# The order of two block products in the feed-forward input units of a two-layer attention and mLSTM kernel

## The chip, the cores and the metric

The kernel runs on one core of a Trainium2 chip. The metric is the device time of one execution in microseconds; less is better. The engines are named as the profile names them: PE is the matrix engine (PEld its weight load), DVE the vector engine, ACT the scalar engine, POOL GpSimd, and SP the engine that issues most DMAs. Matmuls read SBUF and accumulate into PSUM banks; ACT and DVE read the banks.

## The reference

The model has a dilated attention layer and an mLSTM layer over 512 tokens of width 1024, each followed by a gated feed-forward block. The block is what the change touches:

```python
D_FF = -(-8 * D_MODEL // (3 * 256)) * 256        # 2816

def swiglu(xn, w_in, w_out):
    gu = xn @ w_in
    return (jax.nn.silu(gu[..., :D_FF]) * gu[..., D_FF:]) @ w_out

def reference(x, positions, ...):
    h = x
    for i in range(DEPTH):                       # 2
        ...                                      # attention, then mLSTM
        h = h + swiglu(rms_norm(h, ffn_norm[i]), ffn_w_in[i], ffn_w_out[i])
    return rms_norm(h, final_norm)
```

All is in float32, and nothing of the change alters what is computed; the sums of one unit are only formed in another order.

## The kernel before, in words

One program runs the layers one after the other. Names beginning with `f0` and `f1` are the feed-forward input of layer 0 and 1, `o0` and `o1` the out-projections behind them. A float32 product is made of three matmuls of shorter numbers: every operand is split into a high part (`_h`, ACT, L207) and a low part (`_l`, DVE, L208), and high by high, low by high and high by low are added up in the bank.

`ffn_in` computes silu(x w_gate) * (x w_up). After a rest of 256 columns (`f0rest`) come five units, u = 0 to 4, of 512 gate and 512 up columns. The tokens are cut into two halves, and the weights of a unit into four blocks: a11 and a12 make the gate columns, a21 and a22 the up columns, each from one half of the input width. Instead of eight block products a unit has seven, after the manner of Strassen: `PRODUCTS` lists them in the order of their issue. Four of them use sums of weight blocks (s1 to s4, their splits are named `f00s`, the first digit after f being the layer and the next the unit), and T1 to T4 are sums of token blocks that are made once in each layer.

A product is two chunks c of 256 input rows, and in each the two 128-token tiles t, with 6 matmuls for each t: 24 matmuls of 128x512 outputs. Three pairs of PSUM banks, one bank for each t, collect them:

- "c": a11, then a12.
- "p": s1, then s4.
- "u": begun with a copy of a11's sum by ACT (L1222), then s2, s3 and a22.

Only a11 and s1 start their banks anew. Each later product adds on top of what stands there, and each partial sum is wanted by itself. So the sum must be read off a bank before the next product on the same bank may write. `after` does this when a product's last chunk is done: s1 leaves `up` (copy by ACT, L1214), s2 leaves `g2` (copy by ACT, L1214, named `g` in the trace), s4 is folded onto `g2` (DVE, L1217) which then goes through silu (ACT, L1235), s3 is folded onto `up` (DVE, L1217) which is multiplied by `g2` (DVE, L1239) and, in units 0 to 3, transposed in 32x32 blocks by DVE into a tile named `turn` (L1183). The sum after a22 goes with the gate of a12 the same way (L1243). `turn` is then spread into the hidden tile (`hid`): twelve small DMAs by SP (L1194) and four copies by POOL (L1199), which POOL makes after the second L1130 DMA of the next unit.

Weights come in raw tiles two chunks ahead of their products (`AHEAD`, `prepare`). Two tiles per chunk, `first` (block a11) and `own` (a21, onto which POOL's DMA adds a22, L1103), carry all four sums: DVE adds `first` to `own` after the split for s1 (L1129), POOL's accumulating DMA adds a21 to `first` (L1130), which is then s3's operand, and DVE adds a12 to `own` (L1134), which is then s4's. Each tag has two buffers, so the loads of the next unit wait for the last reader of the tiles.

Unit 4 has no `turn`: its rows are turned by PE in the out-projection. `early` does the out-projection's first steps during unit 4, after the products s2, the next two, and a22: B11 forms of the hidden tiles, split by ACT (L1371, `o0B`) and DVE (L1373). Further steps (DVE L1427, ACT L1408) are also put among unit 4's.

Within each engine the order of instructions is fixed when the program is built, by a scheduler that follows the order of the code and its own estimates. So moving a product moves the instructions around it as well.

Of the kernel before, what the change touches and what calls it, by code (L numbers as in the profile page):

```python
# [15 lines left out]
ALU = mybir.AluOpType  # L16
# [54 lines left out]
def tile_hybrid_dilated_attn_mlstm(  # L71
# [4 lines left out]
    nc = tc.nc  # L76
# [64 lines left out]
    def advance():  # L141
        tick[0] += 1
        run_deferred(lambda t: t <= tick[0])
# [200 lines left out]
    with ExitStack() as actx:  # L344
# [62 lines left out]
        banks = [("s", 2), ("s", 2), ("acc", 3), ("acc", 3), ("acc", 3), ("t", 1), ("s", 2), ("s", 2)]  # L407
# [321 lines left out]
        kept = dp.tile([KC, P, SEQ], F32, name="x_kept")  # L729
# [338 lines left out]
        return pair, rbc, r, hook  # L1068


    PRODUCTS = (("a11", "B11"), ("a12", "B21"), ("s1", "T1"), ("s2", "T2"), ("s4", "B22"), ("s3", "T3"), ("a22", "T4"))
    UNITS = D_FF // 512
    AHEAD = 2

# [4 lines left out]
    def ffn_in(layer, fp, x1, x2, pair, r, nr, unit):  # L1079
# [6 lines left out]
        todo = [("rest", None, c) for c in range(KC // 2)] + [  # L1086
            (u, key, c) for u in range(UNITS) for key, _ in PRODUCTS for c in range(2)]
        made, raw, toks = {}, {}, {}
# [78 lines left out]
        def tokens(okey, part, k, t):  # L1167
            if okey[0] == "T":
                return toks[okey][part][:, k, t * P:(t + 1) * P]
            c0 = HALF * (int(okey[2]) - 1) + t * P  # L1170
            return pair[part][4 * (int(okey[1]) - 1) + k][:, c0:c0 + P]

        def bank(tag, bufs, name):
            return ps.tile([P, 512], F32, tag=tag, name=nm + name, bufs=bufs)

        def wide(tag, name, n=512, p=fp):
            return p.tile([P, 512], F32, tag=tag, name=nm + name, bufs=2)[:, :n]
# [9 lines left out]
        def spread(dest, src):  # L1187
            for a, g in itertools.product(range(TB), repeat=2):
                to = dest[32 * g:32 * g + 32, :, a * P:(a + 1) * P]
                of = src[32 * a:32 * a + 32, g].rearrange("p n o j -> p n (o j)")  # L1190
                if a == g:
                    waiting.append((to, of))
                else:
                    nc.sync.dma_start(to, of)  # L1194
# [18 lines left out]
        def after(u, key, banks, t, kept):  # L1213
            copy = lambda to, src, scale: nc.scalar.activation(to, src, AF.Copy, scale=scale)  # L1214

            def fold(to, src, scale):
                nc.vector.scalar_tensor_tensor(to, src, scale, to, op0=ALU.mult, op1=ALU.add)  # L1217
            o = 2 + t
            if key == "a11":
                if t == 0:  # L1220
                    banks["u"] = [bank("o", 2, "u%d_u" % u) for _ in range(2)]
                nc.scalar.activation(banks["u"][t], banks["c"][t], AF.Copy)  # L1222
            elif key == "a12":
                g = kept["g", t] = wide("sq", "u%dg%d" % (u, t), p=npl)
                nc.scalar.activation(g, banks["c"][t], AF.Silu, scale=r[:, t:t + 1])
            elif key == "s1":
                kept["up", t] = wide("up", "u%dup%d" % (u, o))
                copy(kept["up", t], banks["p"][t], nr[:, o:o + 1])
            elif key == "s2":
                kept["g2", t] = wide("g2", "u%dg%d" % (u, o))  # L1230
                copy(kept["g2", t], banks["u"][t], r[:, o:o + 1])
            elif key == "s4":
                g = kept["g2", t]
                fold(g, banks["p"][t], r[:, o:o + 1])
                nc.scalar.activation(g, g, AF.Silu)  # L1235
            elif key == "s3":
                up = kept["up", t]
                fold(up, banks["u"][t], nr[:, o:o + 1])
                nc.vector.tensor_tensor(up, up, kept["g2", t], op=ALU.mult)  # L1239
                store(u, o, up, kept)  # L1240
            else:
                g = kept["g", t]
                nc.vector.scalar_tensor_tensor(g, banks["u"][t], nr[:, t:t + 1], g, op0=ALU.mult, op1=ALU.mult)  # L1243
                store(u, t, g, kept)
                if t == 1 and u < UNITS - 1:
                    dest = fp.tile([P, 4, SEQ], F32, tag="hid%d" % u, name="%shid%d" % (nm, u))
                    hid[2 * u:2 * u + 2] = dest[:, 0:2], dest[:, 2:4]
                    spread(dest, kept["to"])

        def store(u, o, src, kept):  # L1250
            if u == UNITS - 1:
                unit.rows[o] = src
            else:
                if "to" not in kept:
                    kept["to"] = turned(4, "u%dturn" % u)
                turn(kept["to"], o, src, 4)
# [4 lines left out]
        for n, (u, key, c) in enumerate(todo):  # L1261
            prepare(n + AHEAD)
            whl = made.pop(n)
            if u == "rest":
                for o in range(TB):
                    for k in range(2):
                        for a, b in SPLITS:
                            nc.tensor.matmul(accs[o], pair[a][2 * c + k][:, o * P:(o + 1) * P], whl[b][:, k],  # L1268
                                             start=((c, k) == (0, 0) and (a, b) == SPLITS[0]),
                                             stop=((c, k) == (KC // 2 - 1, 1) and (a, b) == SPLITS[-1]))  # L1270
                if c == KC // 2 - 1:
                    rest_out(accs)
            else:
                if (key, c) == ("a11", 0):
                    banks, kept = {}, {}
                name = {"a11": "c", "a12": "c", "s1": "p", "s4": "p"}.get(key, "u")
                fresh = name not in banks
                if fresh:
                    banks[name] = [bank(*{"c": ("acc", 3), "p": ("s", 2)}[name], "u%d_%s" % (u, name)) for _ in range(2)]
                new = key in ("a11", "s1")  # L1280
                for t in range(2):
                    for k in range(2):
                        for a, b in SPLITS:
                            nc.tensor.matmul(banks[name][t], tokens(dict(PRODUCTS)[key], a, 2 * c + k, t), whl[b][:, k],  # L1284
                                             start=(new and (c, k) == (0, 0) and (a, b) == SPLITS[0]),
                                             stop=((c, k) == (1, 1) and (a, b) == SPLITS[-1]), skip_group_check=True)
                if c == 1:
                    for t in range(2):
                        after(u, key, banks, t, kept)
                    if u == UNITS - 1:  # L1290
                        unit.early([k for k, _ in PRODUCTS].index(key))
            advance()
# [684 lines left out]
```

## Time and profile before

| | |
|---|---|
| time, median of 3 runs | 1393.19 us (1391.07 to 1393.89) |
| time of the profiled execution | 1393.05 us |
| its span | 1391.3 us |
| mean granted PE clock | 0.996 |
| PE busy | 1368.8 us (98%) |
| DVE, ACT, POOL busy | 1070.5, 712.4, 221.7 us |
| units of layer 0, of layer 1 | about 500 to 711 us, 1048 to 1269 us |

The span is what the profile shows of the execution; the time includes what lies around it. A row of a timeline reads: start, duration, engine, line, operation, output <- inputs, with the idle time before it and what ended that in brackets. A row of the wait view reads: who waited for whom, us in total, times, longest. A row of the window view reads: stretch, its length, busy time (and instructions) by engine, the granted PE clock (1.00 is full), the busy share of the DMA engines, GB/s.

### The profile page before, as it was taken

The page shows a single profiled execution, that of the slowest core. Times are in us where ns is not written, and L with a number is a line of the kernel's source. Part 1 is how long each engine was busy: PE and PEld are TensorE (multiplying, and loading weights), DVE is VectorE, ACT ScalarE, POOL GpSimd, SP SyncE. Part 2 cuts the span into 40 slices and gives each one's busy share as a digit, 9 for nine tenths or more (in the row PEclk, how much of TensorE's full clock was granted, in tenths as well). Part 3 has the DMA queues.
Part 4 walks back from the last instruction along what each step waited for, and adds up shares of the span by engine and source line. Part 5 has one row for each costly group of instructions (what it writes and reads, how often), then busy time and mean ns, then how long its engine had stood idle before and what let it go on. Part 6 is the DMA issues. An engine that isn't in the chain of part 4 may idle for free. (4 is left out here: it accounts for less than half of the span.)

```text
span 1391.3 us, 18579 instructions
## 1 busy us (share of the span) xinstructions
PE 1368.8 (98%) x6754; PEld 1151.7 (83%) x6754; DVE 1070.5 (77%) x1808; ACT 712.4 (51%) x1165; POOL 221.7 (16%) x241
## 2 busy tenths in 40 slices
PE   9999999999999999999999999999999999999997
PEld 7788888888888888888789988798888888887886
DVE  7976658687797687777997678987757877799665
ACT  7255553332324555555653553985545555566434
POOL 1013201001010202222402010100000222241212
PEclk9999999999999999999999999999999999999999
DMA  9537743527262657767685443322174777778462
GB/s 292 154 83 184 195 128 93 172 76 242 76 204 92 174 136 188 192 176 175 163 241 120 82 122 90 92 62 61 61 196 113 186 187 178 168 167 244 116 136 76
DMA packets 140644, 205.13 MB, mean 147 GB/s; under 512 B 10436, under 2 KB 74500, under 8 KB 140552
## 3 DMA queue, kind: packets, MB, share of 16 engines
q1 hardware_dynamic: 113712, 147.24, 33.5%
q0 software_dynamic: 24608, 54.84, 20.9%
q10 hardware_dynamic: 2232, 1.86, 0.5%
q8 instruction: 53, 0.87, 0.3%
q14 instruction: 39, 0.32, 0.1%
HBM read 183.16 MB, written 10.09 MB: 139 GB/s over the span
## 5 line engine op out<-in xcount | busy, mean ns | idle before, releaser
L523 DVE TENSOR_TENSOR rot<-rot,sinr 32x1024 f32<-32x1024 f32 x24 | 28.9, 1205 | 0.0
L208 DVE TENSOR_TENSOR o1a_l<-o1a_w,o1a_h 128x1024 fp32r<-128x1024 f32 x12 | 14.7, 1223 | 16.0 <-ACT o1a_h L207 16.0
L208 DVE TENSOR_TENSOR o0a_l<-o0a_w,o0a_h 128x1024 fp32r<-128x1024 f32 x12 | 14.7, 1223 | 14.4 <-ACT o0a_h L207 14.4
L207 ACT ACTIVATE o1a_h<-o1a_w 128x1024 fp32r<-128x1024 f32 x12 | 12.7, 1057 | 24.9 <-PE o_acc L1919 8.7
L207 ACT ACTIVATE o0a_h<-o0a_w 128x1024 fp32r<-128x1024 f32 x12 | 12.7, 1057 | 24.9 <-PE o_s L1513 8.7
L238 PE MATMUL mo<-n_h,mo_k_h 128*128 128x512 f32 x64 | 25.4, 396 | 0.0
L238 PE MATMUL mo<-n_h,mo_k_l 128*128 128x512 f32 x64 | 25.2, 394 | 0.0
L238 PE MATMUL mo<-n_l,mo_k_h 128*128 128x512 f32 x64 | 25.2, 394 | 0.0
L238 PE MATMUL awo<-ao_h,awo_k_h 128*128 128x512 f32 x64 | 25.2, 396 | 0.0
L238 PE MATMUL mqk<-n_h,mqk_k_h 128*128 128x512 f32 x64 | 25.1, 392 | 0.0
L238 PE MATMUL mqk<-n_l,mqk_k_h 128*128 128x512 f32 x64 | 25.1, 392 | 0.0
L238 PE MATMUL awo<-ao_l,awo_k_h 128*128 128x512 f32 x64 | 25.0, 390 | 0.0
L238 PE MATMUL mqk<-n_h,mqk_k_l 128*128 128x512 f32 x64 | 25.0, 390 | 0.0
L238 PE MATMUL mwo<-yo_l,mwo_k_h 128*128 128x512 f32 x64 | 24.9, 389 | 0.0
L238 PE MATMUL mwo<-yo_h,mwo_k_l 128*128 128x512 f32 x64 | 24.9, 389 | 0.0
L238 PE MATMUL mwo<-yo_h,mwo_k_h 128*128 128x512 f32 x64 | 24.9, 389 | 0.0
L238 PE MATMUL awo<-ao_h,awo_k_l 128*128 128x512 f32 x64 | 24.9, 391 | 0.0
L1499 PE MATMUL o_acc<-o0B,o0a_h 128*128 128x256 f32 x128 | 23.4, 284 | 0.0
L1499 PE MATMUL o_o<-o0T,o0s_h 128*128 128x256 f32 x128 | 23.4, 285 | 0.0
L1724 POOL CAST ql<-ql 64x512 fp32r<-64x512 f32 x8 | 7.1, 889 | 94.3 <-DVE ql L1723 94.3
L207 ACT ACTIVATE o0s_h<-o0own 128x1024 fp32r<-128x1024 f32 x12 | 12.7, 1058 | 18.2 <-PE o_s L1499 6.3
L1905 PE MATMUL o_acc<-o1a_h,o1B 128*128 128x512 f32 x64 | 20.9, 395 | 0.0
(1841 smaller groups left out, 5142.6 us busy)
## 6 DMA issues: line engine op xcount, KB each, us to landing
o0a_w<-in_ffn_w_out_dram SPq DMA_DIRECT2D x12, 512.0 KB, 3.8
o1a_w<-in_ffn_w_out_dram SPq DMA_DIRECT2D x12, 512.0 KB, 5.9
awo_k_w<-in_attn_w_out_dram SPq DMA_DIRECT2D x8, 512.0 KB, 4.1
o0own<-in_ffn_w_out_dram POOLq DMA_DIRECT2D x8, 512.0 KB, 8.0
mv_k_w<-in_mlstm_w_in_dram SPq DMA_DIRECT2D x8, 512.0 KB, 3.9
mqk_k_w<-in_mlstm_w_in_dram SPq DMA_DIRECT2D x8, 512.0 KB, 3.6
mo_k_w<-in_mlstm_w_in_dram SPq DMA_DIRECT2D x8, 512.0 KB, 3.6
mwo_k_w<-in_mlstm_w_out_dram SPq DMA_DIRECT2D x8, 512.0 KB, 3.5
```

The lines of the kernel that those rows point to most:

```text
L207: nc.scalar.activation(hi[:, :n], raw[:, :n], AF.Copy)
L208: nc.vector.tensor_tensor(lo[:, :n], raw[:, :n], hi[:, :n].bitcast(F32), op=ALU.subtract)
L238: nc.tensor.matmul(acc, whl[a][:, k, m * P:(m + 1) * P], pairs[b][kk], start=(kk == 0 and (a, b) == SPLITS[0]), stop=(kk == nk - 1 and (a, ...
L523: nc.vector.tensor_tensor(sh, sh, sinr.unsqueeze(1).to_broadcast([R, 2, SEQ]), op=ALU.mult)
L1499: nc.tensor.matmul(dst[m // 2][:, (m % 2) * HALF:(m % 2 + 1) * HALF], whl[a][:, k, m * P:(m + 1) * P], unit.form(okey, b, 2 * c + k), star ...
L1724: nc.gpsimd.tensor_copy(ql[oth], ql[own].bitcast(F32))
L1905: nc.tensor.matmul(dst[t], unit.form(okey, a, 2 * c + k)[:, t * P:(t + 1) * P], whl[b][:, k], start=(first and k == 0 and (a, b) == SPLITS ...
```

## The change

In `PRODUCTS` s3 comes ahead of s4, so that the u banks are written by s2 and s3 one after the other, the p banks by s4, and the u banks again by a22. `after` is written to match: the fold of `up` comes with s3, and the multiplication and the store with s4, since they want both.

```diff
-    PRODUCTS = (("a11", "B11"), ("a12", "B21"), ("s1", "T1"), ("s2", "T2"), ("s4", "B22"), ("s3", "T3"), ("a22", "T4"))
+    PRODUCTS = (("a11", "B11"), ("a12", "B21"), ("s1", "T1"), ("s2", "T2"), ("s3", "T3"), ("s4", "B22"), ("a22", "T4"))
...
             elif key == "s2":
                 kept["g2", t] = wide("g2", "u%dg%d" % (u, o))
                 copy(kept["g2", t], banks["u"][t], r[:, o:o + 1])
+            elif key == "s3":
+                fold(kept["up", t], banks["u"][t], nr[:, o:o + 1])
             elif key == "s4":
-                g = kept["g2", t]
+                up, g = kept["up", t], kept["g2", t]
                 fold(g, banks["p"][t], r[:, o:o + 1])
                 nc.scalar.activation(g, g, AF.Silu)
-            elif key == "s3":
-                up = kept["up", t]
-                fold(up, banks["u"][t], nr[:, o:o + 1])
-                nc.vector.tensor_tensor(up, up, kept["g2", t], op=ALU.mult)
+                nc.vector.tensor_tensor(up, up, g, op=ALU.mult)
                 store(u, o, up, kept)
```

Three places show what this makes of the order on the engines. From L1239 on, lines stand one lower in the changed kernel. The first is DVE in layer 0, unit 0, from the fold that comes first to the next unit's second split; `f0u_p` and `f0u_u` are the banks, 4303 and 4305 the two tiles of `up`, 4339 and 4341 those of `g2`. Before:

```order
L1217 SCALAR_TENSOR_TENSOR f0u0g_4339<-f0u_p,n1r,f0u0g_4339 128x512
L1217 SCALAR_TENSOR_TENSOR f0u0g_4341<-f0u_p,n1r,f0u0g_4341 128x512
L208 TENSOR_TENSOR f00a_l<-f00a_w,f00a_h 128x1024 x2
L1217 SCALAR_TENSOR_TENSOR f0u0up_4303<-f0u_u,n1nr,f0u0up_4303 128x512
L1217 SCALAR_TENSOR_TENSOR f0u0up_4305<-f0u_u,n1nr,f0u0up_4305 128x512
L1239 TENSOR_TENSOR f0u0up_4303<-f0u0up_4303,f0u0g_4339 128x512
L1239 TENSOR_TENSOR f0u0up_4305<-f0u0up_4305,f0u0g_4341 128x512
L1183 STREAM_TRANSPOSE f0u0turn<-f0u0up_4303 128x4x4x32
L1183 STREAM_TRANSPOSE f0u0turn<-f0u0up_4305 128x4x4x32
L208 TENSOR_TENSOR f01a_l<-f0u1w_4422,f01a_h 128x1024
L208 TENSOR_TENSOR f01a_l<-f0u1w_4423,f01a_h 128x1024
```

And in the changed kernel:

```order
L1217 SCALAR_TENSOR_TENSOR f0u0up_4303<-f0u_u,n1nr,f0u0up_4303 128x512
L1217 SCALAR_TENSOR_TENSOR f0u0up_4305<-f0u_u,n1nr,f0u0up_4305 128x512
L208 TENSOR_TENSOR f00a_l<-f00a_w,f00a_h 128x1024 x2
L1217 SCALAR_TENSOR_TENSOR f0u0g_4339<-f0u_p,n1r,f0u0g_4339 128x512
L1217 SCALAR_TENSOR_TENSOR f0u0g_4341<-f0u_p,n1r,f0u0g_4341 128x512
L208 TENSOR_TENSOR f01a_l<-f0u1w_4422,f01a_h 128x1024
L1238 TENSOR_TENSOR f0u0up_4303<-f0u0up_4303,f0u0g_4339 128x512
L1238 TENSOR_TENSOR f0u0up_4305<-f0u0up_4305,f0u0g_4341 128x512
L1183 STREAM_TRANSPOSE f0u0turn<-f0u0up_4303 128x4x4x32
L1183 STREAM_TRANSPOSE f0u0turn<-f0u0up_4305 128x4x4x32
L208 TENSOR_TENSOR f01a_l<-f0u1w_4423,f01a_h 128x1024
```

The two pairs of folds have changed places, and the next unit's first low split has gone ahead of the multiplications.

The second place is ACT in layer 0, unit 4, around the copies of s2's sum off the u banks (L1214, `f0u4g`). Before:

```order
L207 ACTIVATE f04s_h<-f0u4w_5317 128x1024
L1214 ACTIVATE f0u4g_5535<-f0u_u,n1r 128x512
L1371 ACTIVATE o0B_2_5809<-f0hid_5360 128x512
L1214 ACTIVATE f0u4g_5537<-f0u_u,n1r 128x512
L207 ACTIVATE f04s_h<-f0u4w_5316 128x1024
```

In the changed kernel:

```order
L207 ACTIVATE f04s_h<-f0u4w_5317 128x1024
L1214 ACTIVATE f0u4g_5535<-f0u_u,n1r 128x512
L1370 ACTIVATE o0B_2_5809<-f0hid_5360 128x512
L1214 ACTIVATE f0u4g_5537<-f0u_u,n1r 128x512
L207 ACTIVATE f04s_h<-f0u4w_5316 128x1024
```

The order is the same, but the split ahead of the copies is now s3's second chunk and the one behind them s4's first; before it was the other way round. The product that writes the u banks next is now the next product and not the one after it.

The third place is PE in layer 1, unit 0, at the beginning of a22 (`f1T4h`); `hT` are transposes of the residual stream after the mLSTM (L304), wanted at the program's end. Before:

```order
L1284 MATMUL f1u_u<-f10s_h,f1T3h 128x512
L1284 MATMUL f1u_u<-f10s_l,f1T3h 128x512
L1284 MATMUL f1u_u<-f10s_h,f1T3l 128x512
L304 MATMUL hT_10888<-cst,hn_6609 128x128
L304 MATMUL hT_10888<-cst,hn_6627 128x128
L304 MATMUL hT_10888<-cst,hn_6618 128x128
L304 MATMUL hT_10888<-cst,hn_6636 128x128
L1284 MATMUL f1u_u<-f10a_h,f1T4h 128x512
```

In the changed kernel:

```order
L1283 MATMUL f1u_p<-f10s_h,n_h_9093 128x512
L1283 MATMUL f1u_p<-f10s_l,n_h_9093 128x512
L1283 MATMUL f1u_p<-f10s_h,n_l_9094 128x512
L1283 MATMUL f1u_u<-f10a_h,f1T4h 128x512
L1283 MATMUL f1u_u<-f10a_l,f1T4h 128x512
```

The four transposes are gone from here, as they are from units 1 and 2 of that layer; all twelve stand in the out-projection `o1` instead.

## The prediction

> **What bounds the kernel now.** I read the page's busy time first, then what PE waits for, then the chain of waits around one unit, then the time of the two products on either side of the edit, unit by unit.
>
> ```profile
> PE 1368.8 (98%) x6754; PEld 1151.7 (83%) x6754; DVE 1070.5 (77%) x1808; ACT 712.4 (51%) x1165; POOL 221.7 (16%) x241
> ```
> ```profile
> PE f0u_u L1284 <- DVE f0u4up L1217: 3.0, 1, 3.0
> PE f1u_u L1284 <- DVE f1u4up L1217: 3.0, 1, 3.0
> ...
> PE f1u_u L1284 <- DVE f1u3up L1217: 0.5, 1, 0.5
> ```
>
> PE is busy 98% of the span, so time is only to be had where PE stands still, or from work taken off it. The two longest waits in the second view are the same place in the two layers: the last product (a22) of unit 4 waits 3.0 us for DVE's fold of `up` off the u banks. The other units have it at up to 0.5 us (unit 3 of layer 1 in the row). The chain shows the ordinary pace, here in the second layer's unit 0:
>
> ```profile
> 1092.41 5.44 PE f1u_p L1284 x24
> 1097.85 5.44 PE f1u_u L1284 x24
> 1103.29 0.44 PE hT L304 x4
> ```
>
> A product is 24 matmuls and 5.44 us. The two u products (s3, then a22) should take 10.88; between them stands a fold. What they took, for units 0 to 4 of layer 0 and then of layer 1, from the first matmul of s3 to the first after a22 (first column the length):
>
> ```profile
> 539.85:551.51 11.66, 11.17 (x49) 1.00 1.04 300
> 578.71:590.35 11.64, 11.15 (x49) 1.00 1.03 305
> 617.55:629.21 11.66, 11.17 (x49) 1.00 1.03 302
> 656.41:668.05 11.64, 11.15 (x49) 1.00 1.01 305
> 695.33:711.13 15.80, 12.77 (x49) 0.89 1.04 287
> 1097.69:1109.33 11.64, 11.59 (x53) 1.00 1.04 304
> 1136.53:1148.18 11.65, 11.61 (x53) 1.00 1.01 299
> 1175.38:1187.04 11.66, 11.61 (x53) 1.00 1.03 304
> 1214.24:1225.88 11.64, 11.14 (x49) 1.00 1.03 304
> 1253.16:1269.26 16.10, 13.09 (x50) 0.89 1.04 294
> ```
>
> Eight units lose 0.76 to 0.78 us, the two units 4 lose 4.92 and 5.22. Three units of layer 1 count 53 matmuls: four transposes (`hT`, 0.44 us) fill their gap. In unit 4 the granted clock (the number before the last two) is 0.89. Cut finer:
>
> ```profile
> 700.28:703.69 3.41, 0.99 (x5) 0.49 (x3) 3.41 (x6) 3.21 (x5) 0.00 (x0) 1.00 1.01 163
> 703.69:707.10 3.41, 2.85 (x7) 2.30 (x8) 3.41 (x6) 0.00 (x0) 0.00 (x0) 0.50 1.09 239
> ...
> 1263.47:1266.88 3.41, 3.41 (x10) 2.63 (x9) 2.67 (x4) 0.02 (x1) 0.00 (x0) 0.50 1.06 331
> ```
>
> PE worked 0.99 of 3.41 us, and the next 3.41 us ran at half the clock. In these about half of 2.85 and of 3.41 is lost, 1.4 and 1.7 us; both lie inside the 4.92 and 5.22.
>
> By the Trainium skill, page "TensorE: Matmul & The Clock Gate", section "Part 1: The HAM clock gate (the "warmup" mystery)", the clock falls after an idle window of about 3.4 us. The length of the slow stretch agrees (3.41), but the stretch ahead of it was not idle, as 0.99 us of it was worked; the row decides, and I count the slow stretch with the stall.
>
> **What goes.** With s4 (banks p) between s3 and a22 (both u), the fold of `up` has s4's 5.44 us to finish in, where it had none. The terms: layer 0, units 0 to 3, 0.78 + 0.76 + 0.78 + 0.76 = 3.08; its unit 4, 4.92. Layer 1, units 0 to 2: 0.76 + 0.77 + 0.78 = 2.31, but their transposes do not vanish, they move to the out-projection behind, so 3 x 0.44 = 1.32 comes back and 0.99 is left. Unit 3, 0.76; unit 4, 5.22. Together 14.97.
>
> **What the new neighbours cost, units 0 to 3.** Now s3 follows s2 on the u banks, so ACT's copy of s2's sum (L1214, named g) must be out before. In layer 0, unit 0, with the product that now stands in s3's place:
>
> ```profile
> 531.94 1.06 ACT L207 ACTIVATE f00s_h<-f0u0w 128x1024 fp32r<-128x1024 f32 x1 [1.13 <-PE f0u_u L1284]
> 533.25 0.69 ACT L1214 ACTIVATE f0u0g<-f0u_u,n1r 128x512 f32<-128x512 f32 x1 [0.25 <-PE f0u_u L1284]
> 534.61 0.69 ACT L1214 ACTIVATE f0u0g<-f0u_u,n1r 128x512 f32<-128x512 f32 x1 [0.67 <-PE f0u_u L1284]
> ```
> ```profile
> 534.41 0.39 PE L1284 MATMUL f0u_p<-f00s_h,n_h 128*128 128x512 f32 x1
> ...
> 535.77 0.39 PE L1284 MATMUL f0u_p<-f00s_h,n_h 128*128 128x512 f32 x1
> ```
>
> The copies end at 533.94 and 535.30; PE comes to the two banks at 534.41 and 535.77. Each copy is 0.47 early, so the wait costs nothing. It is covered because the two t halves are computed one after the other and a copy is short; were ACT 0.47 later, PE would lose what is beyond.
>
> The raw weights of s3 come by an accumulating DMA from POOL (L1130), and they are now read one product, 5.44 us, sooner, at the ACT split just quoted (531.94).
>
> ```profile
> L1130 POOL DMA_DIRECT2D f0u0w<-in_ffn_w_in_dram x2: 1179/1184/1188, 522.9 to 525.3; - x2
> ...
> L1130 POOL DMA_DIRECT2D f0u4w<-in_ffn_w_in_dram x2: 1188/1192/1197, 679.5 to 682.4; - x2
> ...
> DMA to landing us min/median/max: 5.7/6.1/6.9
> ```
>
> Issued at 525.3, the second chunk lands at 531.0 to 532.2, median 531.4: in time by 0.5 at the median, and late by 0.3 at the worst. Behind the split ACT has 0.25 idle and the copy 0.47, so up to 0.7 late is free. Cost 0; from below, no gain is hidden here; from above, the worst landing is free as well.
>
> The fold and multiplication on DVE move: `up` is folded under s4, and the fold of g, silu, multiplication and two transposes come under a22. The durations, from unit 0 of layer 0:
>
> ```profile
> 543.91 1.22 DVE L208 TENSOR_TENSOR f00a_l<-f00a_w,f00a_h 128x1024 fp32r<-128x1024 f32 x1 [1.54 <-ACT f00a_h L207]
> 545.05 1.40 DVE L1217 SCALAR_TENSOR_TENSOR f0u0up<-f0u_u,n1nr,f0u0up 128x512 f32<-128x512 f32 x2
> 546.38 1.28 DVE L1239 TENSOR_TENSOR f0u0up<-f0u0up,f0u0g 128x512 f32<-128x512 f32 x2
> 547.58 1.30 DVE L1183 STREAM_TRANSPOSE f0u0turn<-f0u0up 128x512 f32<-128x512 f32 x2
> ```
>
> The folds, the multiplications, the transposes and one split make 1.40 + 1.28 + 1.30 + 1.22 = 5.2 us. This fits into a22's 5.44, and the split that the next product needs first stands ahead of the multiplications in the new order. Cost 0; without a22's cover it would be up to 5.2 a unit.
>
> **Unit 4** is where I am least sure. There ACT's queue holds, between the two copies of s2's sum, a copy o0B that reads what POOL writes (L1199):
>
> ```profile
> L1199 POOL COPY f0hid<-f0u3turn x4: 607/884/7912, 683.6 to 692.9; 32x512 f32<-32x512 f32 x4
> ```
> ```profile
> 687.69 1.06 ACT L207 ACTIVATE f04s_h<-f0u4w 128x1024 fp32r<-128x1024 f32 x1 [0.54 <-DVE f0u4w L1134]
> 688.73 0.69 ACT L1214 ACTIVATE f0u4g<-f0u_u,n1r 128x512 f32<-128x512 f32 x1
> 692.20 0.63 ACT L1371 ACTIVATE o0B<-f0hid 128x512 fp32r<-128x512 f32 x1 [2.78 <-POOL f0hid L1199]
> 692.74 0.67 ACT L1214 ACTIVATE f0u4g<-f0u_u,n1r 128x512 f32<-128x512 f32 x1
> ```
> ```profile
> 683.49:691.05 7.56, 7.56 (x9) 1.00 0.97 228
> ```
> ```profile
> 687.50 1.21 DVE L208 TENSOR_TENSOR f04s_l<-f0u4w,f04s_h 128x1024 fp32r<-128x1024 f32 x1
> ```
>
> POOL's first copy began at 683.6 and took 7.912 us (the shortest 0.607), while DVE never paused (third fence: DVE alone, busy 7.56 of 7.56). So o0B began at 692.20 and the second g copy ended at 693.41. In the old order only s4's fold wanted it; in the new one s3 wants the bank. By unit 0's distances PE comes to the two banks 1.16 and 2.52 us after the first copy's start, here at 689.9 and 691.3; with nothing else changed the second copy would be 2.1 late. I expect the knot to loosen. The ACT split at 687.69 now belongs to s3, whose second chunk, issued at 682.4, lands at 688.5 (median), so that split ends near 689.6. DVE's lo split behind it, next in DVE's new order, must wait for it from the end of the row last quoted, 688.7. In that pause of 0.9 POOL gets in; its first two copies, 0.6 each, end by 689.9, o0B by 690.9, and the second g copy by 691.5. The first g copy, behind the later split, ends near 690.3. PE thus loses about 0.3 in each unit 4, 0.6 in all; the bounds are 0 and, if POOL is not let in, the 2.1 and the slow clock again.
>
> By the Trainium skill, page "SBUF — State Buffer", section "Who interferes with whom", a DVE instruction with two SBUF inputs and a GpSimd one that reads SBUF exclude each other for one whole instruction. By that, POOL would wait for one DVE operation at most, and the stuck unit 4 among the rivals could not be. The row shows 7.9 us and a train of DVE operations that pass it, so I go by the row and keep that rival.
>
> **The out-projection behind** starts about 8 us sooner than its loads were timed for, and layer 1's takes 12 more transposes with their copies. I take 0.8, between 0 and the 1.32 of the transposes again.
>
> Sum: 14.97 - 0.6 - 0.8 = 13.6. The profiled execution took 1393.05 us (0.14 below the median of the runs, 1393.19), so 1379.5.
>
> **Rivals.** *Unit 4 stays stuck.* POOL finds no pause; the second g copy ends 2.1 us after s3 wants its bank, 2.9 with the later split, and with the slow clock again unit 4 gains about nothing. For: the new wait is on the very queue that stood for 2.78. Against: DVE itself must now pause. 3.08 + 0.99 + 0.76 = 4.83 is left, less 0 to 0.8 behind: 1388.2 to 1389.0, say 1388.5. Chance 0.16.
>
> *The slow clock stays.* It is not owed to the stall but to the mean of these stretches, and 1.4 + 1.7 = 3.1 is not won: 1382.6. Against it: no other unit's two products show it (1.00 in the rows), and PE will not pause there. Chance 0.04. The Trainium skill's clock rule, cited above, speaks for it, as by that rule the worked 0.99 us should have kept the clock up.
>
> *The change doesn't do what it says.* The stall only moves to the out-projection, whose loads and splits are not ready sooner; PE waits there for what it gained. For: unit 4 runs with DVE full. Against: the splits have the same queue and start sooner too. All 13.6 given back makes 1393.05. Chance 0.06.
>
> *Slower.* The DMA of L1130 lands late, and s3 is read 5.44 us sooner in each of ten units. Free up to a landing of 525.3 to 532.6, that is 7.4 us. Accumulating DMAs from POOL in the out-projections need more:
>
> ```profile
> o1own<-in_ffn_w_out_dram POOLq DMA_DIRECT2D x8, 512.0 KB, 9.1
> ```
>
> At 9.1 each unit would lose 1.7, 17 in all, against 13.6 won: 1396.5. It decides from 8.8 on. Against: all twenty landed within 6.9, and nothing else is loaded sooner there. Chance 0.05.
>
> **How the numbers follow.** The forecast, 1379.5, has 0.69; its own range is 1378 (nothing lost) to 1383 (double the losses, some clock). The rivals are 0.16, 0.04, 0.06 and 0.05. Range for 8 in 10: 1377 to 1388.5, with about 1 us below for the spread of runs, and reaching over the stuck unit 4 above. About 0.2%, 2.8 us, is what a measurement of this kernel can tell from no change. Faster 0.69 + 0.16 + 0.04 = 0.89, less 0.01 for a stuck unit 4 that also loses behind: 0.88; same 0.07; slower 0.05.
>
> **What would show it.** In the profile after, the waits of a22 for `up` are gone in all ten units, s3 to s4 to a22 run at 5.44 each, and the granted clock of unit 4 is 1.00. Right on unit 4 is a first POOL copy well under 7.9 us and a PE wait for ACT's g below 0.5. Wrong would be a PE wait of 2 to 3 us for g's copy there, waits for L1130's data in units 0 to 3, or new waits of PE in the first products of the out-projection.

## The result

| | before | after |
|---|---|---|
| time, median (range) | 1392.13 us (1389.82 to 1393.89, 4 runs) | 1382.13 us (1380.99 to 1383.03, 4 runs) |
| time of the profiled execution | 1393.05 us | 1380.99 us |
| its span | 1391.3 us | 1379.2 us |
| mean granted PE clock | 0.996 | 0.998 |

The changed kernel takes 0.9929 of the time, 95% interval 0.9911 to 0.9947: 10.0 us less by the medians, 12.1 by the two profiled executions. The forecast was 1379.5, 13.6 less. The time lies in the range of 1377 to 1388.5 and the direction is right; the gain was forecast too large.

**In the input units.** The window view over the last three products of a unit, s4, s3 and a22 before and s3, s4 and a22 after, from the first matmul of the first to the first matmul behind a22, for units 0 and 4 of layer 0 and then of layer 1 (stretch, length, PE busy and its instructions, clock, DMA share, GB/s). Before:

```profile
534.41:551.51 17.10, 16.61 (x73) 1.00 0.79 221
689.89:711.13 21.24, 18.21 (x73) 0.92 0.89 249
1092.25:1109.33 17.08, 17.02 (x77) 1.00 0.78 222
1247.72:1269.26 21.54, 18.53 (x74) 0.92 0.90 258
```

After:

```profile
533.76:550.08 16.32, 16.32 (x73) 1.00 0.76 224
...
686.18:702.60 16.42, 16.42 (x73) 1.00 0.65 224
1084.76:1101.08 16.32, 16.32 (x74) 1.00 0.76 224
1237.19:1253.67 16.48, 16.48 (x74) 1.00 0.66 221
```

Three products of 5.44 us are 16.32. Units 0 to 3 now take that to the hundredth, but for 0.02 in one of them, and the two units 4 lose 0.10 and 0.16. No wait of a22 for `up` is left in any of the ten units, and the clock is full.

**In unit 4** the knot loosened as forecast. Tile, ACT and DVE rows of layer 0, after:

```profile
L1199 POOL COPY f0hid<-f0u3turn x4: 607/1235/5567, 679.6 to 687.4; 32x512 f32<-32x512 f32 x4
```
```profile
684.47 1.06 ACT L207 ACTIVATE f04s_h<-f0u4w 128x1024 fp32r<-128x1024 f32 x1 [1.02 <-DMA f0u4w<-in_ffn_w_in_dram]
685.43 0.67 ACT L1214 ACTIVATE f0u4g<-f0u_u,n1r 128x512 f32<-128x512 f32 x1
686.20 0.63 ACT L1370 ACTIVATE o0B<-f0hid 128x512 fp32r<-128x512 f32 x1
686.74 0.67 ACT L1214 ACTIVATE f0u4g<-f0u_u,n1r 128x512 f32<-128x512 f32 x1
```
```profile
685.56 1.36 DVE L208 TENSOR_TENSOR f04s_l<-f0u4w,f04s_h 128x1024 fp32r<-128x1024 f32 x1 [0.83 <-ACT f04s_h L207]
```

ACT waits for s3's late weights, DVE pauses 0.83 us for ACT (0.9 was forecast), and POOL's first copy ends after 5.57 us in place of 7.91. The copy o0B that stood for 2.78 us starts without a wait, and the second copy of s2's sum ends at 687.41.

**In the out-projections** a part is given back. From the end of the input units of layer 0 to the first product of layer 1, and from their end in layer 1 to the program's end; before, then after:

```profile
711.13:1070.49 359.36, 356.73 (x2105) 1.00 0.40 107
1269.26:1391.26 122.00, 113.86 (x517) 0.98 0.46 122
```
```profile
702.60:1062.99 360.39, 357.21 (x2105) 1.00 0.42 111
1253.67:1379.21 125.54, 115.48 (x529) 0.98 0.51 133
```

That is 1.03 and 3.54 us more. Of the 3.54, 1.32 are the twelve transposes that moved (529 instructions in place of 517). What PE waits for there, in the wait view after, was not in the profile before, and makes 2.5 us:

```profile
PE hT L304 <- ACT ht L1849: 1.7, 1, 1.7
...
PE o_acc L1512 <- DVE o0p_l L208: 0.5, 1, 0.5
...
PE o_acc L1918 <- ACT ht L1849: 0.3, 1, 0.3
```

ACT's copy `ht` stands in ACT's queue behind a split whose weights are late:

```profile
1260.33 1.06 ACT L207 ACTIVATE o1a_h<-o1a_w 128x1024 fp32r<-128x1024 f32 x1 [3.82 <-DMA o1a_w<-in_ffn_w_out_dram]
1261.29 1.07 ACT L1849 ACTIVATE ht<-hT 128x512 f32<-128x512 f32 x2
```

Why they are late is the question of the experiments. Among what moved with the change are the loads of the out-projection's first two `own` tiles. SP and POOL rows of layer 1, before (its input units end at 1269.26) and after (1253.67):

```profile
1250.41 0.88 SPq L1324 DMA_DIRECT2D o1own<-in_ffn_w_out_dram  x2
```
```profile
1245.63 0.41 SPq L1323 DMA_DIRECT2D o1own<-in_ffn_w_out_dram  x1
...
1249.89 0.46 SPq L1323 DMA_DIRECT2D o1own<-in_ffn_w_out_dram  x1
```
```profile
1251.84 1.19 POOL L1321 DMA_DIRECT2D o1own<-in_ffn_w_out_dram  x1 [12.41 <-DMA o1own<-in_ffn_w_out_dram]
1257.07 1.20 POOL L1321 DMA_DIRECT2D o1own<-in_ffn_w_out_dram  x1 [4.04 <-PE hT L304]
```

These two tiles take the room (tags x4 and x5) of token tiles whose last reader is the first half of s4. Before, that half was over two products ahead of the units' end, and the loads went out 18.9 us ahead of it; now there is one product behind s4, and they go out 8.0 and 3.8 us ahead, the accumulating ones on POOL 1.8 ahead and 3.4 behind. Those two take 9.5 and 9.8 us to land, so they are under way while the out-projection's weights are loaded; before, both had landed when the units ended.

### The profile page after: what moved, and what is told of

It reads as the page before. It is cut to its first block, busy times and chain, and to the rows that moved or that the text cites. A ratio compares the mean times of both kernels' runs of the same rounds, so it can differ in the third digit from the quotient of the medians.

```text
span 1379.2 us, 18574 instructions
## 1 busy us (share of the span) xinstructions
PE 1362.9 (99%) x6754; PEld 1149.5 (83%) x6754; DVE 1070.5 (78%) x1808; ACT 712.3 (52%) x1165; POOL 218.3 (16%) x241
## 5 line engine op out<-in xcount | busy, mean ns | idle before, releaser
L1498 PEld LDWEIGHTS o_acc<-o0B,o0a_h 128*128 128x128 f32 x128 | 20.1, 192 | 0.3
```

Source lines behind the costliest of these rows:

```text
L1498: nc.tensor.matmul(dst[m // 2][:, (m % 2) * HALF:(m % 2 + 1) * HALF], whl[a][:, k, m * P:(m + 1) * P], unit.form(okey, b, 2 * c + k), star ...
```

## The experiments

Times are medians; a difference goes by the runs of before made on the same chip (1392.12 us for l0_only, u4_only, before_no_pool_copies and after_hoist, 1391.88 for after_own_gated, after_both_gated, before_own_gated and late12, 1393.99 for u03_only, u4_own_gated and late6).

### One layer, one kind of unit

The order of products was made to depend on the layer or on the unit (each run has one of the first three lines; `todo`, `after` and `early` then go by `order`):

```diff
+        third_first = lambda u: layer == 0          # l0_only
+        third_first = lambda u: u == UNITS - 1      # u4_only
+        third_first = lambda u: u < UNITS - 1       # u03_only
+        names = [key for key, _ in PRODUCTS]
+        order = lambda u: names if third_first(u) else names[:4] + ["s4", "s3"] + names[6:]
```

> Layer 0 has the new order in all five units, layer 1 the old one. Theory: layer 0's input units end 7.9 us sooner as in the profile after, of which about 1.0 is lost before layer 1 begins; so 6.9 us under before, and layer 1 as it was, its 3.0 us wait and slow clock included. Rival (the layers share the gain evenly, what is lost is lost in both out-projections alike): 5 us under before, with about 3 us lost in the out-projection of layer 0.

Measured: 1385.2 us, ratio 0.996 (0.9948 to 0.9972), 6.9 under before. The theory's number was met, and its profile agrees: the input units of layer 0 are 8.0 us shorter, the out-projection behind them is 1.0 longer, and layer 1 is as before to 0.2.

> Only unit 4 of each layer has s3 ahead of s4; units 0 to 3 keep the order of before. Theory (the gain is the stall, and two thirds of it stood in the two units 4): the stalls of 3.0 us and the slow clock go there, 4.8 and 5.1 us as in the profile after, the 0.5 us waits of units 0 to 3 stay, and the transposes stay in their gaps; with 1 to 2 us lost behind in the out-projections the time is 8 to 9 us under before. Rival (what unit 4 wins is given back by the out-projection, whose loads are not ready sooner): no more than 3 us under before.

Measured: 1389.51 us, ratio 0.9986 (0.9977 to 0.9994), only 2.6 under before. The theory missed, and the rival's number was met. In the profile the input units are 4.7 and 5.0 us shorter, nearly as the theory said, but then the out-projections take 1.7 and 6.4 more. From the wait view, and the clock in windows around that wait:

```profile
PE hT L304 <- ACT ht L1854: 4.2, 1, 4.2
```
```profile
1266.00:1269.40 3.40, 0.90 (x4) 0.93 1.06 363
1269.40:1272.80 3.40, 1.70 (x8) 0.50 1.09 302
```

It is the wait of the changed kernel, longer, and the clock halves behind it. So most of what unit 4's new order wins can be lost behind it, and in the changed kernel a part is.

> Units 0 to 3 have s3 ahead of s4, unit 4 keeps the order of before. Theory (parts add up, and what the out-projections gave back belongs to unit 4's new order alone): eight units at 38.08 in place of 38.85, 6.1 us, less 1.3 for the transposes if they move behind: 4.8 to 6.1 under before, the out-projections as long as before; 1386 to 1387.5. Rival (any sooner arrival at the out-projection is lost there): within 2 us of before.

Measured: 1386.19 us, ratio 0.9949 (0.9936 to 0.9962), 7.8 under before. By the profile units 0 to 3 of layer 0 take 38.08 us each in place of 38.85, and the out-projection of layer 0 is as long as before (359.37); that of layer 1 is 1.4 longer, 0.5 of it a wait for `ht` and 0.9 two groups of transposes that moved there. The theory holds but for that wait. The measured gain is larger than the 4.8 to 6.1 of the units: in this profile layer 1's stall does not bring the slow clock (last section), and by the two profiled executions the gain is 6.6.

### What held unit 4 before

The four diagonal blocks of unit 3's tile went by DMA from SP, the order of products as before:

```diff
-                if a == g:
+                if a == g and not by_dma:           # by_dma: u == UNITS - 2
                     waiting.append((to, of))
```

> The order of before; only the spreading of unit 3's tile is changed: its four diagonal blocks go by four more DMAs from SP in place of POOL's copies, so that ACT's o0B waits for no POOL. Theory (DVE's train holds POOL's copy for 7.9 us, ACT's queue stands behind it, and that is what makes unit 4's wait of 3.0 us): the wait falls to 0.5 us, the slow clock goes, 8.5 us less in the two units 4, 6 to 8 us under before. Rival (unit 4's extra work on DVE and ACT is by itself too much, POOL's copy is only late): the wait stays at 2 to 3 us, the time within 1 us of before.

Measured: 1388.62 us, ratio 0.9979 (0.997 to 0.9988), 3.5 under before. Its wait view:

```profile
PE hT L304 <- ACT ht L1850: 2.5, 1, 2.5
...
PE f1u_u L1284 <- DVE f1u4up L1217: 1.0, 1, 1.0
PE f0u_u L1284 <- DVE f0u4up L1217: 1.0, 1, 1.0
```

The waits of 3.0 fell to 1.0 us and the slow clock went (mean clock 0.999). So POOL's copy made two of the three us, as the first theory had it; the rest is more than the 0.5 of the other units, which the rival's extra work would make. The time misses the theory's 6 to 8 us, because the out-projection of layer 1 took 2.5 us of it back, with the same wait, although here the `own` loads from SP were out 14.9 us ahead. Reaching the out-projection sooner is enough for some of that wait. Its trace has the accumulating `own` transfers under way behind the units' end here too: the second went out 8.9 us ahead of it and took 11.5 us to land. Which transfers are in the way in this kernel was not tested.

### Where the transposes stand

> The changed kernel, with three of the eight groups of transposes (hT) and their ACT copies written behind a22 of units 0 to 2 of layer 1, where the scheduler had put them before, in place of the out-projection. Theory (the out-projection of layer 1 loses 1.7 and 0.3 us since PE waits for ACT's copies of the transposes, which stand in ACT's queue behind a split that waits for its load): both waits go, PE's own 0.44 per group stays, 2 us under the changed kernel, about 1380. Rival (the load is late anyhow and PE would wait for its split instead): within 0.7 us of the changed kernel.

```diff
+        ffn_in(1, ..., lambda u: residual((0, 1, 3)[u], 0) if u < 3 else None)   # called behind a22 of unit u
...
-                for i in (2 * n, 2 * n + 1):
+                for i in ((), (2,), (4, 5), (6, 7))[n]:
```

Measured: 1383.49 us, ratio 0.9947 (0.9935 to 0.9959), 1.4 over the changed kernel's median, though ranges meet (1382.51 to 1385.65). The theory fell. With fewer transposes in the out-projection the wait for `ht` was 2.6 us, for ACT stood even longer behind another late load:

```profile
1267.84 1.06 ACT L207 ACTIVATE o1p_h<-o1p_w 128x1024 fp32r<-128x1024 f32 x1 [7.30 <-DMA o1p_w<-in_ffn_w_out_dram]
```

So the place of the transposes is not what costs the time; the next runs test the loads.

### The loads themselves

The loads of the first two `own` tiles were put behind later loads in SP's queue. In the program the other two `own` tiles take their place, but those go out ahead of the input units either way, in layer 1 at 1048.0 us in the changed kernel and at 1047.3 here. For after_both_gated the loads of `first` were put later too:

```diff
-                if n in (0, 1, 4, 5):
-                    self.load_own((0, 1, 4, 5).index(n))
+                if n in (0, 1):
+                    self.load_own(2 + n)
+                if n in (5, 6):
+                    with tc.issue_after(last_on(mybir.EngineType.SP)):
+                        self.load_own(n - 5)
                 if 5 <= n < 9:
-                    self.load_first(n - 5)
+                    with tc.issue_after(last_on(mybir.EngineType.SP)):    # after_both_gated only
+                        self.load_first(n - 5)
```

> The changed kernel; in the out-projections the loads of the first two own tiles (two from SP, two accumulating ones from POOL) stand in SP's queue behind the loads of p0 and the first of a12, in place of the last product of unit 4 and the first of the out-projection. Theory (what the out-projections give back is a burst of loads: s4, now later, is the last reader of the token tiles whose room the own tiles take, so their loads fall on the first weights of the out-projection, which land in 7.7 to 9.8 us in place of 4): these land in 4 to 6 us, PE's waits of 1.7 and 0.3 us for ACT's copies go, and about 0.5 in layer 0: 2 us under the changed kernel, 1380. Rival (the loads of the firsts alone fill the burst, or SP's buffers set the pace): the waits stay at 1 to 2 us, the time within 0.7 us of the changed kernel.

Measured: 1377.99 us, ratio to before 0.9898 (0.9884 to 0.9911), 4.1 under the changed kernel's median, with no overlap of the runs (1377.79 to 1378.6 against 1380.99 to 1383.03). The out-projections in its profile:

```profile
702.87:1062.28 359.41, 356.81 (x2105) 1.00 0.41 112
1253.80:1376.81 123.01, 115.05 (x529) 0.98 0.51 136
```

The first is as long as before, the second 1.0 longer with 1.32 of transposes more. No wait of PE at their start is left, and the 3.25 us that had been given back are regained. Within the units this profile shows one new wait, 0.6 us in unit 4 of layer 1. By the two profiled executions the gain over the changed kernel is 2.4 us, near the 2 expected; the medians say 4.1, since the profiled execution is the fastest of four there and the slowest of four here. Among the weights that land late after the change are those of layer 0's p0. The DMA view puts them together with p1's, loaded some 80 us later (the last column is the median from issue to landing); in the kernel before, after, and here:

```profile
o0p_w<-in_ffn_w_out_dram SPq DMA_DIRECT2D x6, 512.0 KB, 3.8
```
```profile
o0p_w<-in_ffn_w_out_dram SPq DMA_DIRECT2D x6, 512.0 KB, 9.1
```
```profile
o0p_w<-in_ffn_w_out_dram SPq DMA_DIRECT2D x6, 512.0 KB, 3.6
```

By themselves, p0's loads took 3.7 to 4.7 us before, 9.1 to 10.0 after, and 3.6 to 3.8 here. The only edit was to the order of the `own` loads, so this shows the cause: what the out-projections gave back, they gave back because the transfers of the `own` tiles fell on their first weights. That they did so since s4, now later, frees the room later is read from the issue times: the first of the two goes out at 1245.63, and the first half of s4 ends at about 1245.5. Coming to the out-projection sooner has a part in it too, as before_no_pool_copies lost 2.5 us with loads that were out sooner; how much each part makes was not separated.

> As after_own_gated, and the loads of the four first tiles stand behind those of a12 too. Theory: the burst at the start of the out-projections is gone altogether, all first weights land in about 4 us, no wait of PE there; 2 to 2.5 us under the changed kernel, and at most 0.5 under after_own_gated. Rival (the firsts come too late for s1's sums): a new wait of PE at s1 or s2, slower than after_own_gated by 1 us or more.

Measured: 1377.69 us, ratio to before 0.9895 (0.9881 to 0.9908). The first theory holds, with 0.3 us under after_own_gated, which the ranges hardly tell apart (1377.42 to 1378.08). It is the fastest kernel found.

> The kernel before with the own loads put later in the same way. Theory: before has no wait of PE at the start of the out-projection of layer 1 that they could cause, so nothing is won: within 1 us of before. Rival (these loads also feed the stall of unit 4 itself, through the shared DMA): the 3.0 us waits shrink, 2 us or more under before.

Measured: 1392.74 us, ratio 1.0001 (0.999 to 1.0012). Nothing is won without the change, so the gated loads are worth something only because the change moved them.

> u4_only (s3 ahead of s4 in unit 4 alone) with the own loads put later as in after_own_gated. Theory (u4_only won 4.7 and 5.0 us in the input units and gave 1.7 and 6.4 back, since the own loads fell on the first weights of the out-projections): the give-back goes but for the transposes' own time, so about 9 us under before, 1383. Rival (the out-projection of layer 1 cannot be entered sooner than it was, whatever is loaded when): still within 4 us of before.

Measured: 1383.17 us, ratio 0.9928 (0.9917 to 0.994), 10.8 under before. With the loads out of the way unit 4's new order is worth about what its windows showed (9.4 by the two profiled executions); the out-projections take 359.32 and 121.97 us, as before the change. This settles the miss of u4_only.

### How late may s3's weights be

Twelve and six memsets on POOL were put ahead of the second L1130 transfer in units 0 to 3:

```diff
+                if c == 1 and u < UNITS - 1:
+                    spare = fp.tile([P, 256], F32, tag="spare", ...)
+                    for _ in range(12):             # late6: 6
+                        with tc.issue_after(last_on(mybir.EngineType.Pool)):
+                            nc.gpsimd.memset(spare, 0.0)
```

> The changed kernel, with twelve small memsets on POOL ahead of the second L1130 transfer in units 0 to 3 of both layers, so that it is issued some 2.4 us later (a guess at 0.3 us each). Theory (that landing may be about 1 us later before PE waits, since ACT has 0.25 us to spare and the copies 0.47): each us beyond about 1 costs one us in each of eight units, so at 2.4 us later about 1.4 x 8 = 11 us over the changed kernel, to be read off the landings of the trace. Rival (PE comes to the second chunk only 2.7 us later, so the landing has 3 us to spare): nothing lost.

Measured: 1426.85 us, ratio 1.0249 (1.0224 to 1.0273), 45 over the changed kernel. Layer 0, unit 0: the memsets on POOL, the split on ACT that waits, and s2 with s3 on PE; behind them the same split and window of the changed kernel, whose unit begins 0.91 us sooner.

```profile
524.37 4.38 POOL L1134 MEMSET f0u0spare<- 128x256 f32 x12
```
```profile
535.57 1.06 ACT L207 ACTIVATE f00s_h<-f0u0w 128x1024 fp32r<-128x1024 f32 x1 [4.50 <-DMA f0u0w<-in_ffn_w_in_dram]
```
```profile
529.23:542.82 13.59, 11.17 (x49) 1.00 0.58 148
```
```profile
531.24 1.06 ACT L207 ACTIVATE f00s_h<-f0u0w 128x1024 fp32r<-128x1024 f32 x1 [1.08 <-PE f0u_u L1283]
```
```profile
528.32:539.20 10.88, 10.88 (x49) 1.00 0.58 152
```

The split begins 535.57 - 531.24 - 0.91 = 3.42 us later, and PE loses 13.59 - 10.88 = 2.71. So 0.71 of lateness is free, where the prediction had 0.25 + 0.47 = 0.72. The total was dearer than expected, for two reasons in the trace: the memsets took 4.38 us in place of the guessed 3.6, and from unit 1 on the loss is 5.7 to 6.7 us a unit, with the mean clock at 0.984.

> As late12 with six memsets, which took 0.365 us each there: 2.2 us, so the second L1130 transfer is issued about 1.2 us later than in the changed kernel. Theory (late12's unit 0 landed 3.6 us later and lost 2.7, so 0.9 are free): 0.2 to 0.4 us lost in each of eight units, no slow clock, 2 to 4 us over the changed kernel. Rival (more transfers in the way and the slow clock made late12 dear, and they come with any wait): 8 us or more over the changed kernel.

Measured: 1382.57 us, ratio 0.9923 (0.991 to 0.9935), 0.4 over the changed kernel's median, and the ranges overlap. In the units nothing was lost: they take 190.5 and 190.6 us, as in the changed kernel. (The profile loses 1.9 in the out-projection of layer 1, where the wait for `ht` is 2.5 us and the clock halves behind it.) The transfer landed after 5.7 us here instead of 6.3 and so only 0.6 us later than in the changed kernel (unit 0), inside the free 0.7. The expected 0.2 to 0.4 a unit did not come, and the rival's 8 neither.

## Why the prediction was right, and where it was off

- **The stall as the gain (right).** The terms of what goes summed to 14.97, less 0.6 for unit 4. The input units measured 198.48 - 190.60 = 7.88 in layer 0 and 198.77 - 190.68 = 8.09 in layer 1; less the 1.32 of transposes that only moved, 14.65, against 14.37 forecast.
- **The copies of s2's sum (right).** They cost nothing in units 0 to 3. The margin is real: late12 measured 0.71 us.
- **L1130's transfer (right).** The rival *slower* did not come. late12 shows that it would have, with transfers some 3 us later. The price of a late landing was even set too low, as the slow clock joins.
- **Unit 4 (right in mechanism, the size smaller).** DVE's pause let POOL in; 0.10 and 0.16 us lost, where 0.3 each was forecast. The rival *unit 4 stays stuck* did not come. before_no_pool_copies shows that POOL's copy made two of the three us of unit 4's wait.
- **The out-projection behind (the step that failed).** The prediction took 0.8 us, "between 0 and the 1.32 of the transposes again". Measured: 1.03 in layer 0, and 3.54 - 1.32 = 2.22 in layer 1, 3.25 together. The prediction had counted every move on PE, ACT and DVE, but did not price the two `own` loads and their accumulating DMAs, which the order of SP shows moved past the firsts' loads. s4 is the last reader of the tiles they load into; moving it later by one product put four transfers of 512 KB later, and two of them among the first weights of the out-projection. The prediction's own sign of being wrong there, new waits of PE in the first products of the out-projection, is what the profile shows. The rival *the change doesn't do what it says* named the place, the out-projection's loads, but took it for all or nothing.
- **The sum (consistent).** 14.65 - 3.25 is 11.40; the changed kernel's input units also began 0.65 sooner (512.00 against 512.65). No part of the change explains that, and it is luck: the profiles of the thirteen kernels begin these units anywhere from 511.67 to 512.91. Together that is 12.05, as far as the two profiled executions are apart (12.06). The medians differ by 10.0.
- **The clock (a term taken as certain).** The two slow stretches were counted at 1.4 and 1.7 us. They are in the profile of before, but not in every execution: of the 23 executions of before made on the chip of l0_only, the six with a mean granted clock of 0.999 took 1389.63 to 1390.03 us, the five with 0.995 took 1393.44 to 1393.98. So what the change wins depends on the executions of before that it is held against. The medians are 2.1 us less apart than the profiled executions. Of this, 0.9 is how far the profiled execution of before lies above its median, which the clock may explain. The other 1.1 is how far that of the changed kernel lies below its own, which the clock does not explain: it is 0.998 there and 0.999 in the three slower ones.

## What to carry to other kernels

Before a product is moved, list what it is the last reader of: the loads that wait for that room move too, and their price is paid where they land, perhaps in the next stage. A stall that goes is worth its length only if the stage behind can start sooner; look at what its first loads share the DMA with, and put loads that are not urgent behind those that are. Here a few lines on the order of the loads were worth 4.1 us by the medians on top of the change's 10.

## What was not expected of the hardware

A stall of the same length halved the clock in one place and not in another. In late6 and in before_no_pool_copies PE waits 2.5 us for `ht` in the out-projection of layer 1; windows around that wait and behind it, first late6:

```profile
1260.24:1263.65 3.41, 0.92 (x6) 1.00 1.07 344
1263.65:1267.06 3.41, 3.41 (x18) 0.50 1.10 267
```
```profile
1266.80:1270.21 3.41, 0.95 (x6) 1.00 0.71 244
1270.21:1273.62 3.41, 3.41 (x26) 1.00 0.66 231
```

PE worked 0.92 of 3.41 us in the one and 0.95 in the other, and only the first was followed by half the clock. In u03_only unit 4 keeps its old order in both layers, with a wait for `up` of 3.0 us in layer 0 and 2.5 in layer 1, where four transposes fill part of the gap. From the first matmul of s4 to the first behind a22, layer 0 and then layer 1:

```profile
686.06:707.32 21.26, 18.27 (x73) 0.92 0.86 248
1241.59:1261.25 19.66, 17.12 (x78) 1.00 0.87 235
```

The Trainium skill, "TensorE: Matmul & The Clock Gate", section "Part 1: The HAM clock gate (the "warmup" mystery)", says that the window in which activity is judged runs freely and does not start with the kernel; by that the same stall may or may not be seen as idle, and these rows agree, though none of the windows was without work. It would also spread the times of a kernel that has such stalls. Of before_own_gated's twelve executions, the six with a mean clock of 0.995 took 1393.33 to 1394.02 us and the four with 0.998 or 0.999 took 1389.49 to 1389.66; after_own_gated's four, without such stalls, took 1377.79 to 1378.6. How much work a window may hold and still be judged idle was not measured.

The second is how dear shared DMA is for a single load: loads of 512 KB, p0's weights, that took 3.7 to 4.7 us before took 9.1 to 10.0 after the change, when they shared the DMA with one another and with three more of that size, the two accumulating ones of the `own` tiles and one of `first`.
